# Attention's reciprocal row sums sent through DRAM, and the output copied and scaled in two separate steps

## The chip, the core and the metric

The kernel runs on one core of a Trainium2 chip. The metric is the device time of one execution in microseconds (us). The core's engines are named as a profile names them: PE is TensorE (PEld its weight loads), DVE is VectorE, ACT is ScalarE, POOL is GpSimd, SP is SyncE, which only issues transfers here. Each engine works through its own list of instructions in order and waits on semaphores for the others. A transfer is issued by SP or by POOL, and then runs on the 16 DMA engines of the core.

## What is computed

One layer of a hybrid network over 1024 latent tokens of width 1024 and 256 context tokens: a half-step feed-forward, then a short convolution and a grouped-query attention in parallel, merged through gates, then a second feed-forward. The change lies in the attention, where 8 query heads of width 128 share 2 key and value heads:

```python
def gqa_attend(q, k, v):
    s = jnp.einsum('btkgd,blkd->bkgtl', q, k, preferred_element_type=jnp.float32) * (HEAD_DIM ** -0.5)
    p = jax.nn.softmax(s, axis=-1).astype(v.dtype)
    return jnp.einsum('bkgtl,blkd->btkgd', p, v)
...
    k_all = jnp.concatenate([k_c, k_l], axis=1)
    v_all = jnp.concatenate([v_c, v_l], axis=1)
    o_l = latent_attention(q_l, k_all, v_all)

    x = x + ml[5] * merge_branches(y_conv_l, o_l, gt_l, w_branch_conv[layer],
                                   w_branch_attn[layer], w_out[layer])
```

Each query attends to 256 + 1024 = 1280 keys. The softmax's division by the row sum may be done after the product with the values, and so it is here.

## The kernel before

**Products in three parts.** Everything is float32. A factor is split into a high part and a rest (`split`: ScalarE writes the rounded high part with a cast, VectorE, or GpSimd where it is named, subtracts it for the rest), and each product is three matmuls, high x high, high x rest, rest x high.

**Units.** The attention runs in 16 units: 8 heads times two chunks of 512 queries (`C0`, `C1`). A unit has four query tiles (`qt`) of 128 queries. `scores` makes the scores of one tile in three PSUM banks (512 + 512 latent keys, 256 context keys), VectorE takes their maxima (`m3`, then `nm`), ScalarE the exponentials with the row sums as a by-product (into `pl` and `pc`), and VectorE adds the three part sums into one column of `rsum`. So after the fourth tile `rsum` holds 128 x 4 row sums, one query on each partition.

**Values.** The second half of a unit has ten key tiles (`kt`) of 128 keys. `turn(kt)` transposes four 128 x 128 blocks of exponentials on TensorE into one PSUM bank, and `split` makes `pts` of it. `values(kt)` multiplies it with the value tile and adds up in the PSUM bank `po` over all ten tiles. The result has the head's 128 dimensions on the partitions and the 512 queries along the row, so that scaling it takes the reciprocal sums as a row, the same on all partitions.

**The output, as it was.** `output` takes the reciprocals of `rsum` (`rinv`, 128 x 4), spreads them into rows by four transposes on TensorE of a broadcast column (into a PSUM bank of the same kind that `turn` uses), copies `po` to SBUF on ScalarE (`of`), multiplies `of` by that bank on VectorE, and splits the product into the operand `o` of the later branch product.

**What sets the order.** The loop at the end of the stage (`for n, u in enumerate(units)`) interleaves three threads on TensorE: the scores of unit n, in eight half steps; the turns and values of unit n - 1 (`seconds`, one `rest` a step, with values three turns behind, `AHEAD = 3`); and filler products of the convolution and merge branches (`fillers`, `FILLS` steps per unit). While `in_order[0]` is set, TensorE keeps exactly this order. The other engines' lists are set by a scheduler with a cost model of its own, which takes what is ready by its times. The last value product of a unit falls into the fifth half step of the unit after next; between it and the next unit's first value product stand one filler step and one turn.

**Buffers.** `t` banks of PSUM: two, shared by the turns and (before) the spread reciprocals. `po`: one. Row tiles in SBUF (`ttile`, 512 wide): eleven, for queries, gates, `of` and others. Weights of the fillers are loaded to `raw` (three), cast by ScalarE, and subtracted by GpSimd into `wc`; the next weight load on SyncE's list waits for a free `raw`. Query loads (`o<-qd`) stand on the same list, and GpSimd subtracts for the rest of the queries as well (`qs`).

Of the kernel before, what the change touches and what calls it, by code (L numbers as in the profile page):

```python
# [9 lines left out]
F32 = mybir.dt.float32  # L10
# [8 lines left out]
P = 128  # L19
# [7 lines left out]
NQ = 8  # L27
# [24 lines left out]
def tile_dit_layer(  # L52
# [29 lines left out]
    class Engine:  # L82


        def __init__(self, engine):
            self.engine = engine
# [10 lines left out]
    act, dve, pool, pe, sp = (Engine(e) for e in (nc.scalar, nc.vector, nc.gpsimd, nc.tensor, nc.sync))  # L97
# [7 lines left out]
    dram = ctx.enter_context(tc.tile_pool(name="dram", bufs=1, space=DRAM))  # L105
# [3 lines left out]
    def uniq(s):  # L109
        n_tiles[0] += 1  # L110
        return f"{s}_{n_tiles[0]}"

    def atile(name, shape=(P, SLOT), dt=F32):
        return apool.tile(list(shape), dt, tag="A", name=uniq(name))

    def ttile(name, n=512, dt=F32):
        t = tpool.tile([P, 512], dt, tag="t", name=uniq(name))
        return t[:, :n]

    def small(name, n, dt=F32):  # L120
        return spool.tile([P, n], dt, tag=f"s{n}_{name}", name=uniq(name))

    def ps_s(n=512):
        return psum.tile([P, 512], F32, tag="s", name=uniq("ps"), bufs=5)[:, :n]

    def ps_t(n=512):
        return psum.tile([P, 512], F32, tag="t", name=uniq("pt"), bufs=2)[:, :n]

    def ps_o(n=512):
        return psum.tile([P, 512], F32, tag="o", name=uniq("po"), bufs=1)[:, :n]  # L130

    def matmul(out, w, x, start, stop, pinned=False, on=False):

        inst = pe.matmul(out, w, x, start=start, stop=stop, skip_group_check=on)
        if pinned or in_order[0]:
            tc.keep_in_program_order(inst)

    def transpose(out, in_, pinned=False):
        n = in_.shape[0]
        inst = pe.transpose(out, in_, ident[:n, :n])  # L140
        if pinned or in_order[0]:
            tc.keep_in_program_order(inst)
# [37 lines left out]
    def col(name, k=0):  # L180
        o = voff[name] + k
        return cols[:, o : o + 1]
# [8 lines left out]
    def split(src, hi, lo, lo_eng=None, hi_eng=None):  # L191

        if hi_eng is dve:
            dve.tensor_copy(out=hi, in_=src)
        else:
            act.copy(out=hi, in_=src)
        (lo_eng or dve).tensor_sub(out=lo, in0=src, in1=hi.bitcast(F32))
# [25 lines left out]
    def mm3(ps, terms, k0=0, k1=None):  # L223

        last = len(terms) - 1
        for i, (wh, wl, xh, xl) in list(enumerate(terms))[k0:k1]:
            matmul(ps, wh, xh, start=(i == 0), stop=False)
            matmul(ps, wh, xl, start=False, stop=False)
            matmul(ps, wl, xh, start=False, stop=(i == last))
# [565 lines left out]
    class OutColumns(Winograd):  # L795
# [71 lines left out]
        def seconds(self, j):  # L867

            u, v = self.uc[j]
            b = ttile("b")  # L870
            dve.tensor_add(out=u, in0=u, in1=self.product(6))
            dve.tensor_add(out=v, in0=u, in1=self.product(7))
            dve.tensor_sub(out=b, in0=v, in1=self.product(4))
            return b
# [268 lines left out]
    def scaled(k, pt):  # L1143
        act.copy(out=xs(k, C0), in_=pt)
        dve.tensor_mul(out=h0[k % 4][:, k // 4], in0=pt, in1=pr)
# [18 lines left out]
    pr = ttile("pr")  # L1164
# [200 lines left out]
    for j in range(NH):  # L1365
# [3 lines left out]
        u, c = half1.next_first()  # L1369
# [109 lines left out]
    for i in range(KD):  # L1479
        u = atile("u")  # L1480
# [5 lines left out]
        for ch, bg, gc in mixed():  # L1486
# [3 lines left out]
            o = ch[1]  # L1490
            y = ttile("y")
            dve.tensor_scalar(out=y, in0=u[:, o : o + 512], scalar1=col("w1", i), scalar2=None, op0=ALU.mult)
            for j in (0, 2):
# [3 lines left out]
                    out=ya, in0=u[:, a + j - 1 : b + j - 1], scalar=col(f"w{j}", i), in1=ya, op0=ALU.mult, op1=ALU.add  # L1497
# [135 lines left out]
    def v_tile(kt):  # L1633
        if kt < 2:
            return v_ctx[:, kt], v_ctx[:, 2 + kt]
        return tuple(t[:, (kt - 2) % 4] for t in v_lat[(kt - 2) // 4])
# [194 lines left out]
    queries, o_parts = {}, {}  # L1831
# [46 lines left out]
    def conv_out(ch, j):  # L1878
# [10 lines left out]
        sp.dma_start(out=zd[j, :, o : o + 512], in_=g)  # L1889
        yield  # L1890

    class Unit:
        def __init__(self, hd, ch):
            self.hd, self.ch, self.g = hd, ch, hd // (NQ // NKV)
# [11 lines left out]
        def scores(self, qt):  # L1906

            g = self.g
            qh, ql = (t[:, qt * P : (qt + 1) * P] for t in self.qs)
            m3, nm, rs = small("m3", 3), small("nm", 1), small("rs", 3)  # L1910
            pl, parts = atile("pl"), []
            self.pl.append(pl)

            def keys(n, k, dst):
                ps = ps_s(n)
                mm3(ps, [(qh, ql, *k)])
                dve.reduce_max(out=m3[:, len(parts) : len(parts) + 1], in_=ps, axis=AX.X)
                parts.append((dst, ps))

            keys(512, [t[:, :512] for t in k_lat[g]], pl[:, :512])  # L1920
            yield
            keys(512, [t[:, 512:] for t in k_lat[g]], pl[:, 512:])
            keys(CT, [k_ctx[:, 2 * g + v] for v in range(2)], self.pc[:, qt])
            i = 8 * (self.hd // 2 * 2 + self.ch[1] // 512) + 4 * (self.hd % 2) + qt
            y = q_scale[:, i : i + 1]
            dve.tensor_reduce(out=nm[:], in_=m3[:], axis=AX.X, op=ALU.max, negate=True)
            dve.tensor_mul(out=nm[:], in0=nm[:], in1=y)
            for j, (dst, ps) in enumerate(parts):
                act.activation(out=dst, in_=ps, func=AF.Exp, bias=nm[:], scale=y, accum_out=rs[:, j : j + 1])
            dve.reduce_sum(out=self.rsum[:, qt : qt + 1], in_=rs[:], axis=AX.X)  # L1930
            yield

        def turn(self, kt):
# [6 lines left out]
            split(pt, pts[:, 0], pts[:, 1])  # L1940
            return pts

        def values(self, kt, pts):
            if kt == 0:
                self.po = ps_o()
            po = self.po
            vh, vl = (v[:, self.g * HD : (self.g + 1) * HD] for v in v_tile(kt))
            matmul(po, vh, pts[:, 0], start=(kt == 0), stop=False)
            matmul(po, vh, pts[:, 1], start=False, stop=False)
            matmul(po, vl, pts[:, 0], start=False, stop=(kt == 9))  # L1950

        def output(self):
            rinv = small("rinv", 4)
            of, o = ttile("of"), o_parts[self.hd, self.ch]
            dve.reciprocal(out=rinv[:], in_=self.rsum[:])
            pr = ps_t()
            for qt in range(4):
                transpose(pr[:, qt * P : (qt + 1) * P], rinv[:, qt : qt + 1].to_broadcast([P, P]))
            act.copy(out=of, in_=self.po)
            dve.tensor_mul(out=of, in0=of, in1=pr)  # L1960
            split(of, o[:, 0], o[:, 1])

    def seconds():

        turned = []

        def value():
            u, kt, pts = turned.pop(0)
            u.values(kt, pts)
            if kt == 9:  # L1970
                u.output()

        for u in units:
            for kt in range(10):
                turned.append((u, kt, u.turn(kt)))
                if len(turned) > AHEAD:
                    value()
                yield
        while turned:
            value()  # L1980
            yield

    merged = OutColumns([tuple(w_out[0][:, d * P : (d + 1) * P] for d in (e, e + 1)) for e in range(0, KD, 2)])

# [41 lines left out]

    units = [Unit(hd, ch) for ch in (C0, C1) for hd in range(NQ)]
    rest, fill = seconds(), fillers()
    in_order[0] = True
    for n, u in enumerate(units):  # L2030
# [155 lines left out]
    for j in range(NH):  # L2186
        if j > 1:
            run(late_steps, 3)
        u, c = fast.next_first()
# [76 lines left out]
```

## Time and profile before

| What | us |
|---|---|
| Median of 3 runs | 2643.44 (2640.8 to 2643.78) |
| The profiled execution | 2642.17 |
| Its span, first to last instruction | 2640.4 |
| PE busy | 2593.3 (98%) |
| DVE busy | 2072.1 (78%) |
| ACT busy | 1207.4 (46%) |
| POOL busy | 545.1 (21%) |

In a row of the order of time the columns are the start, the length, the engine, the line in the code, the operation, output<-inputs, sizes, and the number of equal instructions that were merged. In brackets stands how long the engine was idle before it, and what it waited for. Nearly all instructions carry line 90, since one helper issues them; they are told apart by the names of their tiles. Matmuls overlap, and a row of several is as long as from the first start to the last end, so distances on PE are read from start to start. In a row by tile the three durations are the shortest, the median and the longest in ns.

### The profile page before, as it was taken

To read this page: it belongs to the slowest core of one execution; us is meant where nothing else is said; L and a number is where in the kernel's file an instruction comes from. 1 tells how busy PE (TensorE), PEld (TensorE's weight loads), DVE (VectorE), ACT (ScalarE), POOL (GpSimd) and SP (SyncE) were. 2 spreads that over 40 slices of the span, in tenths; PEclk is the share of its full clock that TensorE was granted. 3 is DMA by queue.
4 is the path that set the end of the run, shared out by engine and by line. 5 is a ranking of instruction groups with operands and counts; after the bars stand their busy time and mean duration, and the time that the engine had idled before them with its cause. 6 is when DMAs were issued, how large, how long until landed. Compare 5 with 4: busy or idle time off the path is not lost.

```text
span 2640.4 us, 36969 instructions
## 1 busy us (share of the span) xinstructions
PE 2593.3 (98%) x13313; PEld 2189.6 (83%) x13313; DVE 2072.1 (78%) x3463; ACT 1207.4 (46%) x2388; POOL 545.1 (21%) x374
## 2 busy tenths in 40 slices
PE   8999999999999999999999999999999999999998
PEld 5788998888788878888998788888887888888888
DVE  5888879887887899888687766677788777667885
ACT  5623543233444643323456666666447423334444
POOL 1144011121110044232310011111030443321110
PEclk9999999999999999999999999999999999999999
DMA  8665754437974345444536222122434664227851
GB/s 271 223 188 175 231 157 137 128 108 265 292 173 116 116 158 173 135 128 127 176 116 216 88 69 72 55 70 69 138 110 136 195 185 138 88 76 271 215 104 65
DMA packets 373456, 393.08 MB, mean 149 GB/s; under 512 B 16655, under 2 KB 255385, under 8 KB 373273
## 3 DMA queue, kind: packets, MB, share of 16 engines
q1 hardware_dynamic: 364248, 373.43, 44.1%
q0 software_dynamic: 9024, 17.30, 4.1%
q8 instruction: 104, 1.70, 0.3%
q14 instruction: 80, 0.65, 0.1%
HBM read 313.07 MB, written 77.59 MB: 148 GB/s over the span
## 4 chain that ended last, share of the span: by engine, by line
PE 84%; DVE 8%; ACT 4%; DMA 2%; issue 2%; POOL 0%; SPq 0%; DVEq 0%; POOLq 0%; ACTq 0%
PE ps L90 70%; PE po L90 8%; PE pt L90 7%; ACT pl L90 1%; DVE pts L90 1%; DVE r L90 1%; DMA raw<-in_ffn_w_in_dram 1%; DVE wl L90 1%; DVE m L90 1%; ACT r L90 0%; ACT pts L90 0%; ACT wl L90 0%; DVE v L90 0%; DVE u L90 0%; DMA xtok<-in_ctx_dram 0%
## 5 line engine op out<-in xcount | busy, mean ns | idle before, releaser
L90 PE MATMUL ps<-r,wl 128*128 128x512 f32 x5496 | 1267.6, 390 | 8.6 <-DVE wl L90 3.5
L90 PEld LDWEIGHTS ps<-r,wl 128*128 128x128 f32 x5496 | 1026.6, 188 | 223.4 <-DVE wl L90 5.0
L90 ACT CAST wl<-s 128x512 fp32r<-128x512 f32 x266 | 164.4, 620 | 371.4 <-PE ps L90 258.1
L90 ACT CAST wl<-raw 128x512 fp32r<-128x512 f32 x298 | 184.1, 620 | 236.4 <-PE ps L90 140.3
L90 DVE TENSOR_TENSOR wl<-raw,wl 128x512 fp32r<-128x512 f32 x296 | 215.1, 730 | 70.4 <-ACT wl L90 69.2
L90 POOL TENSOR_TENSOR s<-raw 128x512 f32<-128x512 f32 x68 | 98.5, 1448 | 792.5 <-DMA raw<-in_ffn_w_in_dram 384.7
L90 DVE TENSOR_TENSOR wl<-s,wl 128x512 fp32r<-128x512 f32 x266 | 231.0, 870 | 22.4 <-ACT wl L90 21.2
L90 POOL TENSOR_TENSOR s<-raw,s 128x512 f32<-128x512 f32 x68 | 102.6, 1508 | 369.3 <-DVE wl L90 361.4
L90 DVE TENSOR_REDUCE m<-ps 128x1 f32<-128x512 f32 (+1 forms) x192 | 111.0, 596 | 59.3 <-PE ps L90 59.1
L90 DVE SCALAR_TENSOR_TENSOR macc<-rawm,silu_c,macc 128x512 f32<-128x512 f32 x168 | 141.8, 860 | 8.5 <-DMA rawm<-in_w_mod_dram 8.0
L90 DVE TENSOR_TENSOR u<-u,ps 128x512 f32<-128x512 f32 x183 | 124.3, 679 | 26.1 <-PE ps L90 25.9
L90 ACT CAST pts<-pt 128x512 fp32r<-128x512 f32 x160 | 93.6, 587 | 101.7 <-PE pt L90 101.1
L90 PE MATMUL ps<-tw,r 128*128 128x256 f32 x1008 | 125.2, 285 | 3.7 <-DVE tw L90 3.5
L90 DVE TENSOR_TENSOR pts<-pt,pts 128x512 fp32r<-128x512 f32 x160 | 109.5, 685 | 23.8 <-ACT pts L90 21.6
L90 PEld LDWEIGHTS ps<-tw,r 128*128 128x128 f32 x1008 | 122.2, 192 | 4.8 <-DVE tw L90 4.7
L90 ACT CAST rh<-hid 128x512 fp32r<-128x512 f32 x132 | 80.9, 620 | 95.1 <-PE ps L90 86.1
L90 PE MATMUL ps<-rh,wl 128*128 128x512 f32 x360 | 122.0, 389 | 0.0
L90 PE MATMUL po<-pts,v 128*128 128x512 f32 x384 | 120.0, 422 | 0.0
L90 ACT ACTIVATE pl<-ps,nm,qscale 128x512 f32<-128x512 f32 x128 | 98.6, 775 | 43.5 <-DVE nm L90 43.2
L90 POOL TENSOR_TENSOR s<-raw,raw 128x512 f32<-128x512 f32 x74 | 111.6, 1508 | 8.1 <-issue 2.7
L90 PE MATMUL ps<-kl,qs 128*128 128x512 f32 x384 | 110.3, 395 | 2.9 <-ACT pl L90 2.7
L90 PE MATMUL ps<-y,wc 128*128 128x512 f32 x384 | 105.3, 395 | 1.9 <-DVE g L90 1.9
(366 smaller groups left out, 4630.8 us busy)
## 6 DMA issues: line engine op xcount, KB each, us to landing
raw<-in_ffn_w_in_dram SPq DMA_DIRECT2D x128, 512.0 KB
raw<-in_ffn_w_out_dram SPq DMA_DIRECT2D x72, 512.0 KB
rawm<-in_w_mod_dram SPq DMA_DIRECT2D x128, 256.0 KB
raw<-in_w_in_dram SPq DMA_DIRECT2D x53, 512.0 KB
hid<-hd SPq DMA_DIRECT2D x40, 512.0 KB
ws<-in_ffn_w_out_dram POOLq DMA_DIRECT2D x30, 512.0 KB, 6.4
ucd<-uc SPq DMA_DIRECT2D x26, 512.0 KB
hd<-c SPq DMA_DIRECT2D x39, 256.0 KB
```

What stands on the lines that cost most here:

```text
L90: inst = getattr(self.engine, name)(*args, **kw)
```

## The change

Three things change. The reciprocals are taken at the end of a unit's scores, and GpSimd stores the 512 numbers to DRAM, into a row of `rsd`, in the order of the queries. At the unit's fifth value step GpSimd fetches this row back to all 128 partitions (`inv`). `output` only copies `po`, and the multiplication and the split are written two value steps later (`scaled`, at `kt == 1` of the next unit), with `inv` in SBUF as the second operand. The four transposes and their bank are not used any more.

```diff
+    rsd = dram.tile([NQ, 2, 512], F32, name="rsd")
...
             dve.reduce_sum(out=self.rsum[:, qt : qt + 1], in_=rs[:], axis=AX.X)
+            if qt == 3:
+                rinv = small("rinv", 4)
+                dve.reciprocal(out=rinv[:], in_=self.rsum[:])
+                pool.dma_start(out=rsd[self.hd, self.ch[1] // 512].rearrange("(t p) -> p t", p=P), in_=rinv[:])
...
+        def fetch_inverse(self):
+            self.inverse = ttile("inv")
+            pool.dma_start(out=self.inverse, in_=rsd[self.hd, self.ch[1] // 512].partition_broadcast(P))
...
         def output(self):
-            rinv = small("rinv", 4)
-            of, o = ttile("of"), o_parts[self.hd, self.ch]
-            dve.reciprocal(out=rinv[:], in_=self.rsum[:])
-            pr = ps_t()
-            for qt in range(4):
-                transpose(pr[:, qt * P : (qt + 1) * P], rinv[:, qt : qt + 1].to_broadcast([P, P]))
-            act.copy(out=of, in_=self.po)
-            dve.tensor_mul(out=of, in0=of, in1=pr)
+            self.of = ttile("of")
+            act.copy(out=self.of, in_=self.po)
+
+        def scaled(self):
+            of, o = self.of, o_parts[self.hd, self.ch]
+            dve.tensor_mul(out=of, in0=of, in1=self.inverse)
             split(of, o[:, 0], o[:, 1])
...
-        turned = []
+        turned, ended = [], []
 
         def value():
             u, kt, pts = turned.pop(0)
+            if kt == 4:
+                u.fetch_inverse()
             u.values(kt, pts)
             if kt == 9:
                 u.output()
+                ended.append(u)
+            elif kt == 1 and ended:
+                ended.pop().scaled()
...
         while turned:
             value()
             yield
+        ended.pop().scaled()
```

The order on the engines, as built. TensorE at the fourteenth output, before: the last value product (`po`), the spread reciprocals (`pt` from `rinv`), a filler product (`ps`), the next turn.

```order
L90 MATMUL po_17587<-pts_17753,v_13346 128x512 x2
L90 MATMUL po_17587<-pts_17753,v_13347 128x512
L90 MATMUL pt_17841<-ident,rinv_17838 128x128 x4
L90 MATMUL ps_17728<-o_14801,wc_17256 128x512 x2
L90 MATMUL ps_17728<-o_14801,wc_17257 128x512
L90 MATMUL pt_17853<-ident,pl_17424 128x128
```

The same place with the change:

```order
L90 MATMUL po_17562<-pts_17736,v_13346 128x512 x2
L90 MATMUL po_17562<-pts_17736,v_13347 128x512
L90 MATMUL ps_17711<-o_14796,wc_17243 128x512 x2
L90 MATMUL ps_17711<-o_14796,wc_17244 128x512
L90 MATMUL pt_17826<-ident,pl_17409 128x128
```

The four transposes are gone, and the rest of TensorE's list in the stage is as it was. VectorE at the same output, before: the split of the turn ahead (`pts`), the scaling, the split of the output (`o`), the split of the next turn, two maxima of the scores.

```order
L90 TENSOR_TENSOR pts_17832<-pt_17827,pts_17832 128x512
L90 TENSOR_TENSOR of_17839<-of_17839,pt_17841 128x512
L90 TENSOR_TENSOR o_17030<-of_17839,o_17030 128x512
L90 TENSOR_TENSOR pts_17858<-pt_17853,pts_17858 128x512
L90 TENSOR_REDUCE m_3195_17818<-ps_17865 128x1
L90 TENSOR_REDUCE m_3195_17818<-ps_17870 128x1
```

With the change:

```order
L90 TENSOR_TENSOR pts_17815<-pt_17810,pts_17815 128x512
L90 TENSOR_TENSOR of_17821<-of_17821,inv_17669 128x512
L90 TENSOR_TENSOR pts_17831<-pt_17826,pts_17831 128x512
L90 TENSOR_REDUCE m_3198_17801<-ps_17838 128x1
L90 TENSOR_TENSOR o_17009<-of_17821,o_17009 128x512
L90 TENSOR_REDUCE m_3198_17801<-ps_17843 128x1
```

The scaling keeps its place, with the fetched row as its second operand, and the output's split goes behind the next turn's split and a maximum; on ScalarE the cast of `o` goes behind the cast of `pts` likewise. GpSimd around the sixth and seventh unit, before: the rests of the queries (`qs`) and of the fillers' weights (`wc`).

```order
L90 TENSOR_TENSOR qs_15382<-o_15379,qs_15381 128x512
L90 TENSOR_TENSOR wc_15289<-raw_15287,wc_15288 128x1024
L90 TENSOR_TENSOR qs_15654<-o_15651,qs_15653 128x512
L90 TENSOR_TENSOR wc_15508<-raw_15506,wc_15507 128x1024
L90 TENSOR_TENSOR qs_15928<-o_15925,qs_15927 128x512
```

With the change:

```order
L90 TENSOR_TENSOR qs_15373<-o_15370,qs_15372 128x512
L90 DMA inv_15473<-rsd 128x512
L90 DMA rsd<-rinv_15448 128x4x1
L90 TENSOR_TENSOR wc_15290<-raw_15288,wc_15289 128x1024
L90 TENSOR_TENSOR qs_15643<-o_15640,qs_15642 128x512
L90 DMA inv_15754<-rsd 128x512
L90 TENSOR_TENSOR wc_15507<-raw_15505,wc_15506 128x1024
L90 DMA rsd<-rinv_15720 128x4x1
L90 TENSOR_TENSOR qs_15915<-o_15912,qs_15914 128x512
```

In every unit a fetch stands right behind a `qs`, and a store follows, behind the fetch or behind a `wc`. SyncE's list is the same as before.

## The prediction

> **What bounds the kernel now.** I read the chain that ended last first, then the busy times by stage, then the order of time around one of the sixteen places that the change touches.
>
> ```profile
> PE 84%; DVE 8%; ACT 4%; DMA 2%; issue 2%; POOL 0%; SPq 0%; DVEq 0%; POOLq 0%; ACTq 0%
> ```
>
> TensorE (PE) carries 84% of the chain; GpSimd (POOL) and all queues carry nothing. Next the attention stage and all behind it (start:end, length, then busy us and count of PE, PEld, DVE, ACT, POOL, granted clock, DMA share, GB/s):
>
> ```profile
> 1430.00:1867.00 437.00, 423.99 (x2271) 348.52 (x2270) 307.72 (x653) 279.90 (x640) 60.84 (x32) 1.00 0.22 71
> 1867.00:2640.00 773.00, 762.31 (x3532) 636.26 (x3530) 587.03 (x889) 320.26 (x557) 171.96 (x122) 1.00 0.50 147
> ```
>
> In the stage TensorE idles 437.00 - 423.99 = 13 us, VectorE (DVE) 129, ScalarE 157; the clock is full and the DMA engines are 22% busy. So the stage ends when TensorE is through its list, and what is saved there is handed on: in the 773 us behind it TensorE idles 10.7 us only. Where TensorE stands still for others shows at an output; this is the fourteenth:
>
> ```profile
> 1827.55 0.60 PE L90 MATMUL pt<-ident,rinv 128*128 128x128 f32 x4
> 1827.91 0.94 PE L90 MATMUL ps<-o,wc 128*128 128x512 f32 x3
> 1828.12 0.61 ACT L90 COPY of<-po 128x512 f32<-128x512 f32 x1
> 1828.27 0.69 DVE L90 TENSOR_TENSOR pts<-pt,pts 128x512 fp32r<-128x512 f32 x1 [0.32 <-ACT pts L90]
> 1829.02 0.66 PE L90 MATMUL pt<-ident,pl 128*128 128x128 f32 x4 [0.17 <-DVE pts L90]
> 1829.43 0.94 PE L90 MATMUL po<-pts,vc 128*128 128x512 f32 x3
> ```
>
> The four `rinv` transposes take one of the two `t` banks, so the next turn (`pt<-ident,pl`) must wait for the bank of the turn before, which VectorE frees at 1828.96. The third output has no such wait:
>
> ```profile
> 1535.78 0.60 PE L90 MATMUL pt<-ident,rinv 128*128 128x128 f32 x4
> 1536.13 0.94 PE L90 MATMUL ps<-y,wc 128*128 128x512 f32 x3
> 1536.91 0.60 PE L90 MATMUL pt<-ident,pl 128*128 128x128 f32 x4
> 1537.27 0.96 PE L90 MATMUL po<-pts,vc 128*128 128x512 f32 x3
> ```
>
> From start to start: 0.35 us for the transposes, 0.78 for the filler, 0.36 for the turn, 1.49 in all. The fourteenth output takes 1.88, so 0.39 us goes into the bank, more than the 0.17 that the row names as idle.
>
> **Part one, the transposes go.** Alone they are worth 16 x 0.355 = 5.7 us:
>
> ```profile
> L90 PE MATMUL pt<-ident,rinv x64: 270/273/273, 1479.7 to 1867.1; 128*128 128x128 f32 x64
> ```
>
> With the bank also free, the next value product can begin 0.78 + 0.36 = 1.14 us after the old start of the transposes, unless ScalarE's copy of `po` (one bank) is late. I allow 0.05 us between the copy's end and TensorE. Fourteenth output: the copy ends at 1828.73, 1.18 in, so 1.23 instead of 1.88: 0.65 saved. The fourth is the first of eight of this kind (numbers 4, 5, 6, 8, 10, 12, 13 and 14; the last is shown above):
>
> ```profile
> 1562.48 0.60 PE L90 MATMUL pt<-ident,rinv 128*128 128x128 f32 x4
> 1562.94 0.61 ACT L90 COPY of<-po 128x512 f32<-128x512 f32 x1
> 1564.25 0.94 PE L90 MATMUL po<-pts,vc 128*128 128x512 f32 x3
> ```
>
> Here 1.77 becomes 1.14: 0.63. Eight times 0.64 is 5.1 us. Outputs 3, 15 and 16 lose only the transposes: 3 x 0.35 = 1.05. The first two outputs:
>
> ```profile
> 1479.73 0.60 PE L90 MATMUL pt<-ident,rinv 128*128 128x128 f32 x4
> 1481.34 0.60 ACT L90 COPY of<-po 128x512 f32<-128x512 f32 x1
> 1482.77 0.94 PE L90 MATMUL po<-pts,vc 128*128 128x512 f32 x3
> 1507.57 0.60 PE L90 MATMUL pt<-ident,rinv 128*128 128x128 f32 x4
> 1510.25 0.58 ACT L90 COPY of<-po 128x512 f32<-128x512 f32 x1
> 1510.88 0.97 PE L90 MATMUL po<-pts,vc 128*128 128x512 f32 x3 [1.43 <-ACT of L90]
> ```
>
> The first goes from 3.04 to 2.26 (the copy's end plus 0.05): 0.78. The second already waits for the copy: nothing. So far 5.1 + 1.05 + 0.78 = 6.9 us.
>
> Outputs 7, 9 and 11 stay open. There TensorE stands still twice soon after the output:
>
> ```profile
> 1643.31 2.72 DVE L90 TENSOR_TENSOR o<-of,o 128x512 fp32r<-128x512 f32 x1 [0.76 <-POOL qs L90]
> 1643.08 2.40 POOL L90 TENSOR_TENSOR wc<-raw,wc 128x1024 fp32r<-128x1024 f32 x1
> 1647.37 0.63 PE L90 MATMUL pt<-ident,pl 128*128 128x128 f32 x4 [0.92 <-DVE pts L90]
> 1649.84 0.96 PE L90 MATMUL ps<-kl,qs 128*128 128x512 f32 x3 [0.44 <-ACT pl L90]
> 1700.97 0.66 PE L90 MATMUL pt<-ident,pl 128*128 128x128 f32 x4 [0.64 <-DVE pts L90]
> 1703.65 0.96 PE L90 MATMUL ps<-kl,qs 128*128 128x512 f32 x3 [0.63 <-ACT pl L90]
> 1754.93 0.63 PE L90 MATMUL pt<-ident,pl 128*128 128x128 f32 x4 [1.03 <-DVE pts L90]
> 1757.40 0.96 PE L90 MATMUL ps<-kl,qs 128*128 128x512 f32 x3 [0.45 <-ACT pl L90]
> ```
>
> In the new order VectorE does `pts` ahead of `o`, which should end the first wait of each pair. The second hangs on the sum of VectorE's work up to the exponentials, which is the same as before. Their own savings are 0.35 + 0.65 + 0.35 = 1.35, the six waits 4.1: between 0 and 5.5. If the second wait takes everything back, nothing is left; I take about a third, 1.7, nearer to the 1.35.
>
> **Part two, 32 transfers are added on GpSimd.** The nearest rows:
>
> ```profile
> L90 POOL DMA_DIRECT2D ws<-in_ffn_w_out_dram x36: 1194/1222/1442, 682.0 to 2541.1; - x36
> DMA to landing us min/median/max: 5.6/6.5/10.1
> L90 DVE RECIPROCAL rinv<-rsum x16: 166/178/182, 1441.4 to 1842.5; 128x4 f32<-128x4 f32 x16
> 1615.00 0.61 ACT L90 COPY of<-po 128x512 f32<-128x512 f32 x1
> 1616.21 1.30 POOL L90 TENSOR_TENSOR qs<-o,qs 128x512 fp32r<-128x512 f32 x1 [10.13 <-ACT qs L90]
> SPq L90 <- POOL wc L90: 146.0, 17, 20.1
> ```
>
> An issue costs GpSimd 1.2 us: 32 x 1.2 = 39 us beside 61 busy ones in a stage of 437. A store of 512 single numbers is not in the trace; I take 1.2 us too, by the nearest row, up to a few times that at worst. The fetch stands behind `qs`: in the unit of the sixth output (the two rows with a time) it issues near 1617.5 and lands, at the longest landing of 10.1, by 1629. Outputs are (1867.1 - 1479.7) / 15 = 25.8 us apart, so it is used near 1615.6 + 25.8 = 1641.4: 12 us to spare. The last store can issue after 1842.5, its fetch waits for it, and two landings of 6.5 with two issues of 1.2 end at 1858, before output 16. Cost 0.
>
> The store is the wait that is added on GpSimd: it waits for the reciprocal, and where a `wc` subtraction is next in the list, that starts up to 1.2 us later. SyncE's next weight load waits for `wc` (last row), and the next query load stands behind it. These loads are for a later unit, and that cover hides the push; without it ScalarE, which has the query's split in its list ahead of `pts`, would stand still for up to 1.2 us in that unit.
>
> **Part three, the product moves and changes its operand.** `of*inv` stands in VectorE's list where `of*pt` stood, so it hides as before, 0.68 us. It reads two SBUF operands now instead of SBUF and PSUM:
>
> ```profile
> L90 DVE TENSOR_TENSOR of<-of,pt x16: 677/677/689, 1482.8 to 1869.5; 128x512 f32<-128x512 f32 x16
> L90 DVE TENSOR_TENSOR o<-of,o x16: 677/1290/2892, 1485.4 to 1870.9; 128x512 fp32r<-128x512 f32 x16
> L90 DVE TENSOR_TENSOR wl<-ws,wl x35: 682/686/693, 749.9 to 2546.1; 128x512 fp32r<-128x512 f32 x35
> ```
>
> The form with PSUM is never stretched; `o`, of two SBUF operands beside GpSimd's subtractions, is, by 0.6 us in the median and 2.2 at most; beside GpSimd's DMA issues (`wl<-ws,wl`) nothing is. At the sixth output GpSimd begins `qs` 0.6 us after the copy's end, when `of*inv` would have begun; I take 0, with 0 to 1.3 us (one `qs`) per output as the bounds, and 16 x 1.3 = 20.8 us in all.
>
> **Sum.** 6.9 + 1.7 = 8.6 us. The profiled execution took 2642.17 us (span 2640.4, 1.8 around it): 2642.2 - 8.6 = 2633.6. The median of the three runs is 2643.44, 1.3 more, inside their own spread of 3 us.
>
> **Rivals.**
> - The saving is taken back within the unit: the score products still wait for ScalarE's exponentials and VectorE's maxima, as the second waits above do, and a TensorE that is 0.64 us early waits 0.64 us longer. For it: the second output gains nothing, for just that reason. Against it: VectorE idles 129 us in the stage, and only a few waits of this kind show. Between none and half of the sum is left: 2638 to 2642.
> - Slower: `of*inv` and GpSimd lock each other out. If `qs` or `wc` is running at most outputs when the copy ends, the product waits for its end, and `pts`, the maxima and so the turns stand behind it. At 1.3 us on the path at each output this is 2642.2 - 8.6 + 20.8 = 2654.4; it decides from 8.6 / 16 = 0.54 us each. For it: the stretched `o` rows. Against it: GpSimd is busy for 61 of the stage's 437 us, and with `pts` ahead of `o` one SBUF pair less stands before the next turn. The Trainium skill (SBUF — State Buffer, section SBUF: two separate sides) says that a VectorE operation with two SBUF inputs and a GpSimd operation that reads SBUF share a port pair, and that the one which starts first holds it for its whole instruction. The trace agrees: the `o` that began at 1643.31 ended at 1646.03, about one normal length after the end of the `wc` of 1643.08.
> - The fetch is late: four-byte stores so slow that the inverse lands more than 12 us after the time above. Then VectorE stands still at every output, by 16 times the excess: 2 us excess gives 2665. The order of instructions excludes that the transposes stay or that the fetch is issued only at the output.
> - More: all waits at outputs 7, 9 and 11 go, and others like them: 13 us or more, below 2629.
>
> **Chances.** Forecast 0.67 (2629 to 2638), taken back 0.18, locked out 0.08, late 0.03, more 0.04. A measurement tells 0.2%, some 5.3 us, from no change: faster is below 2638.2, slower above 2648.7. Faster 0.67 + 0.04 = 0.71; same 0.18 + 0.02 of mild lock-outs = 0.20; slower 0.06 + 0.03 = 0.09. The range 2629 to 2641 holds the forecast and most of the taken-back case, and leaves out 0.04 + 0.08 + 0.03 and 0.04 at that case's far end.
>
> **What the profile will show.** Right: from the last value product of a unit to the next unit's first, some 0.35 us less at three outputs and 0.6 at eight; `of<-of,inv` near 0.68 us; the stage shorter by 7 to 10 us and the rest unchanged. Wrong: `of<-of,inv` with a mean over 1.2 us, a DMA wait in front of it, waits on `pl` or `pts` that grow, or query loads that land later.

## The result, and the profile after

| | us |
|---|---|
| Before, median of 4 runs | 2642.61 (2640.80 to 2643.78) |
| With the change, median of 4 runs | 2655.88 (2654.01 to 2661.21) |
| Ratio | 1.0055, 95% interval 1.0043 to 1.0067 |
| Profiled execution with the change, its span | 2655.56, 2653.6 |

The change makes the kernel 13 us slower. The forecast was 2633.6 with a range of 2629 to 2641, so the time lies outside it, on the other side of no change.

Chain of waits of the changed kernel, by engine and by line:

```profile
PE 82%; DVE 7%; DMA 5%; ACT 3%; issue 2%; SPq 1%; POOL 0%; DVEq 0%; ACTq 0%; POOLq 0%
PE ps L90 69%; PE po L90 7%; PE pt L90 6%; DMA o<-qd 2%; DVE wl L90 1%; DVE r L90 1%; DMA g<-gcd 1%; DMA raw<-in_ffn_w_in_dram 1%; DMA rawm<-in_w_mod_dram 1%; SPq L90 1%; ACT pl L90 1%; DVE m L90 1%; DVE pts L90 0%; DVE u L90 0%; DMA y<-yd 
```

DMA went from 2% to 5%, and the query loads (`o<-qd`) stand in the chain. Two stretches of the changed kernel (start:end, length, then busy us and count of PE, PEld, DVE, ACT, POOL, granted clock, DMA share, GB/s), the stage as it was cut before and up to its own last output copy:

```profile
1430.00:1867.00 437.00, 411.66 (x2136) 337.89 (x2135) 295.51 (x639) 270.62 (x624) 80.44 (x62) 0.98 0.33 79
1430.00:1881.20 451.20, 425.86 (x2212) 349.57 (x2211) 304.94 (x652) 278.65 (x637) 80.99 (x63) 0.98 0.33 78
```

The kernel before, up to its last output copy:

```profile
1430.00:1867.80 437.80, 424.79 (x2276) 349.23 (x2275) 308.52 (x654) 280.70 (x640) 60.84 (x32) 1.00 0.22 70
```

The stage alone is 13.4 us longer, which is the whole difference. TensorE idles 25.3 us in it instead of 13.0, and it is 1.1 us longer busy although 64 transposes are gone: its clock is granted at 0.98. The DMA engines are 33% busy instead of 22% while they move 78 GB/s instead of 70, so half as much time again goes for a tenth more bytes.

The added transfers (shortest, median and longest issue in ns; landing in us; the first two rows are the store):

```profile
L90 POOL DMA_DIRECT2D rsd<-rinv x16: 755/766/826, 1440.9 to 1856.9; - x16
DMA to landing us min/median/max: 8.6/9.7/11.6
...
L90 POOL DMA_DIRECT2D inv<-rsd x16: 552/567/600, 1455.9 to 1867.9; - x16
L90 DVE TENSOR_TENSOR of<-of,inv x16: 680/684/1908, 1485.0 to 1882.9; 128x512 f32<-128x512 f32 x16
...
DMA to landing us min/median/max: 3.3/3.7/8.1
```

Two KB need 9.7 us to land; the fetch of 256 KB needs 3.7. Now one such store and the loads beside it (order of time of the changed kernel, around the sixth output; the engine is the third column):

```profile
1610.72 0.76 POOL L90 DMA_DIRECT2D rsd<-rinv  x1 [9.93 <-DVE rinv L90]
...
1613.93 0.38 SPq L90 DMA_DIRECT2D raw<-in_w_branch_conv_dram  x1
1614.41 0.53 SPq L90 DMA_DIRECT2D o<-qd  x1
...
1625.38 0.62 ACT L90 CAST qs<-o 128x512 fp32r<-128x512 f32 x1 [2.57 <-DMA o<-qd]
...
1629.63 0.78 ACT L90 ACTIVATE pl<-ps,nm,qscale 128x512 f32<-128x512 f32 x1 [2.14 <-DVE nm L90]
...
1630.55 0.96 PE L90 MATMUL ps<-kl,qs 128*128 128x512 f32 x3 [1.24 <-ACT pl L90]
```

The same stretch in windows of 1 us (last two columns: DMA share, GB/s):

```profile
1612.00:1613.00 1.00, 1.00 (x8) 0.91 (x7) 0.94 (x3) 0.39 (x1) 1.00 (x1) 1.00 0.18 2
...
1616.00:1617.00 1.00, 1.00 (x6) 0.79 (x6) 0.16 (x1) 0.86 (x3) 0.00 (x0) 1.00 0.01 2
...
1618.00:1619.00 1.00, 1.00 (x6) 0.83 (x5) 1.00 (x3) 0.59 (x1) 0.00 (x0) 1.00 0.63 60
1619.00:1620.00 1.00, 1.00 (x6) 0.84 (x5) 0.61 (x3) 0.32 (x1) 0.00 (x0) 1.00 0.52 28
...
1621.00:1622.00 1.00, 1.00 (x6) 0.82 (x6) 0.51 (x2) 1.00 (x5) 0.00 (x0) 1.00 0.71 24
...
1623.00:1624.00 1.00, 1.00 (x5) 0.83 (x6) 0.65 (x2) 0.00 (x0) 0.00 (x0) 1.00 1.09 332
1624.00:1625.00 1.00, 1.00 (x9) 0.92 (x8) 0.00 (x0) 0.00 (x0) 0.00 (x0) 1.00 1.02 380
```

In the kernel before, the same weight load and query load (order of time of SyncE):

```profile
1606.10 0.38 SPq L90 DMA_DIRECT2D raw<-in_w_branch_conv_dram  x1
1606.58 0.53 SPq L90 DMA_DIRECT2D o<-qd  x1
```

and its windows of 1 us:

```profile
1607.00:1608.00 1.00, 1.00 (x8) 0.86 (x7) 0.57 (x1) 1.00 (x3) 0.00 (x0) 1.00 0.45 110
1608.00:1609.00 1.00, 1.00 (x6) 0.82 (x5) 0.12 (x1) 1.00 (x4) 0.00 (x0) 1.00 0.99 301
1609.00:1610.00 1.00, 1.00 (x7) 0.82 (x6) 0.20 (x2) 0.66 (x3) 0.00 (x0) 1.00 1.11 366
```

Before, the loads run at 300 GB/s within two us of their issue and are through by 1611. With the change they are issued at 1613.9 to 1614.9, and the core moves 60 GB/s or less until 1622. The store began at 1610.72 and, at the median landing, was through at 1620.4. Its own 2 KB are the 2 GB/s in the window from 1612, two us after its issue; what takes long comes behind that, up to the landing. So the store does not only take long itself: the transfers beside it nearly stand still. ScalarE then waits at the query's split (`qs<-o`), the exponentials (`pl`) behind it in its list come late, and TensorE waits for them. The waits in 1430 to 1860 of the changed kernel (who, for what, us, times, longest):

```profile
ACT qs L90 <- DMA o<-qd: 20.3, 7, 4.0
PE ps L90 <- ACT pl L90: 11.6, 9, 2.6
...
ACT y L90 <- DMA y<-yd: 7.6, 5, 3.1
PE po L90 <- ACT of L90: 6.2, 2, 4.2
```

And of the kernel before:

```profile
PE pt L90 <- DVE pts L90: 5.2, 10, 1.3
ACT qs L90 <- DMA o<-qd: 4.3, 3, 2.7
...
PE ps L90 <- ACT pl L90: 2.7, 5, 0.6
...
PE po L90 <- ACT of L90: 1.4, 1, 1.4
```

The longer waits cost twice. After the wait for `pl` of 2.64 us that ends at 1658.75, the column ahead of the DMA share, the granted clock, goes down in the changed kernel:

```profile
1659.00:1660.00 1.00, 1.00 (x7) 0.73 (x7) 0.25 (x1) 1.00 (x4) 0.00 (x0) 1.00 0.21 61
1660.00:1661.00 1.00, 1.00 (x8) 0.90 (x7) 0.97 (x4) 0.21 (x2) 0.00 (x0) 0.65 0.06 16
1661.00:1662.00 1.00, 1.00 (x4) 0.81 (x3) 0.77 (x3) 1.00 (x3) 0.00 (x0) 0.50 0.00 0
1662.00:1663.00 1.00, 1.00 (x3) 0.66 (x3) 0.10 (x1) 1.00 (x5) 0.00 (x0) 0.50 0.00 0
1663.00:1664.00 1.00, 1.00 (x6) 0.94 (x5) 0.33 (x2) 0.45 (x2) 0.00 (x0) 0.64 0.00 0
```

TensorE is busy again, but at half clock for 3.4 us. This comes with four waits of the changed kernel, of 4.17, 1.99, 2.64 and 1.74 us (with the first it begins within the wait and lasts 6.8 us), and with none of those of 1.31 us or less. One minus the clock, added up over these stretches of the stage, comes to 8.5 us with the change and to 0 before.

### The profile page after: what moved, and what is told of

Its sections match the earlier page's. It is cut to its first block, busy times and chain, and to the rows that moved or that the text cites. A ratio compares the mean times of both kernels' runs of the same rounds, so it can differ in the third digit from the quotient of the medians.

```text
span 2653.6 us, 36915 instructions
## 1 busy us (share of the span) xinstructions
PE 2594.4 (98%) x13249; PEld 2191.1 (83%) x13249; DVE 2070.4 (78%) x3463; ACT 1206.4 (45%) x2388; POOL 567.0 (21%) x406
## 4 chain that ended last, share of the span: by engine, by line
PE 82%; DVE 7%; DMA 5%; ACT 3%; issue 2%; SPq 1%; POOL 0%; DVEq 0%; ACTq 0%; POOLq 0%
PE ps L90 69%; PE po L90 7%; PE pt L90 6%; DMA o<-qd 2%; DVE wl L90 1%; DVE r L90 1%; DMA g<-gcd 1%; DMA raw<-in_ffn_w_in_dram 1%; DMA rawm<-in_w_mod_dram 1%; SPq L90 1%; ACT pl L90 1%; DVE m L90 1%; DVE pts L90 0%; DVE u L90 0%; DMA y<-yd 0%
## 5 line engine op out<-in xcount | busy, mean ns | idle before, releaser
L90 ACT CAST pts<-pt 128x512 fp32r<-128x512 f32 x160 | 93.7, 587 | 93.1 <-PE pt L90 92.6
```

The lines of the kernel that those rows point to most:

```text
L90: inst = getattr(self.engine, name)(*args, **kw)
```

## The experiments

In the first four, theory S is the one just read from the trace; P, F and O are its rivals: pushed lists, the fetch, the new order on ScalarE and VectorE. All times are medians; the kernel before measured 2642.75 beside the first four, 2642.30 beside the second four, 2641.63 beside experiments 9, 11 and 12, and 2642.31 beside experiment 10. Waits are those in 1430 to 1860 where nothing else is said.

**1. The same store, in 16-byte pieces.**

```diff
-   pool.dma_start(out=rsd[self.hd, self.ch[1] // 512].rearrange("(t p) -> p t", p=P), in_=rinv[:])
+   pool.dma_start(out=rsd[self.hd, self.ch[1] // 512].rearrange("(p t) -> p t", p=P), in_=rinv[:])
...
-   dve.tensor_mul(out=of, in0=of, in1=self.inverse)
+   by_tile = lambda a, s: a.rearrange(s, t=4)
+   dve.tensor_mul(out=by_tile(of, "q (t p) -> q t p"), in0=by_tile(of, "q (t p) -> q t p"),
+                  in1=by_tile(self.inverse, "q (p t) -> q t p"))
```

> The changed kernel, with the row sums' reciprocals stored in the order in which they lie in SBUF: each partition writes its four numbers as 16 contiguous bytes (128 pieces in place of 512 of 4 bytes), and the product reads the inverse through a strided view that puts the columns right. When the store issues, what it waits for and the order on every engine stay. Theory S (the 512 four-byte pieces occupy the DMA engines, the query loads beside them land late, and ScalarE stands at the query's split): the store lands in about 3 to 5 us instead of 9.7, ScalarE's wait for the query load falls from 20.3 us to about the 4.9 of before, and the time to about 2634, the forecast; anything from 2630 to 2640 bears it out. Theory P (GpSimd stands at the store until the reciprocal is there, so its subtraction and with it SyncE's next loads issue late): that wait is unchanged, 2654 to 2657. Theory F (the fetch of 256 KB): unchanged, 2654 to 2657. Theory O (the new order on ScalarE and VectorE costs): 2654 to 2657, or more if the strided read is slow; the product's row, 0.68 us, tells.

Measured: 2637.89, ratio 0.9982 (0.9973 to 0.9991) to the kernel before, 18 us below the changed kernel. Store, its landing, and the product in this run:

```profile
L90 POOL DMA_DIRECT2D rsd<-rinv x16: 543/552/624, 1441.6 to 1837.3; - x16
...
DMA to landing us min/median/max: 1.7/1.7/4.2
...
L90 DVE TENSOR_TENSOR of<-of,inv x16: 1062/1085/2310, 1482.2 to 1863.4; 128x512 f32<-128x512 f32 x16
...
ACT qs L90 <- DMA o<-qd: 4.8, 3, 2.3
```

The landing falls from 9.7 to 1.7 us, the query wait from 20.3 to 4.8, and the clock in the stage is 1.00 again. Bytes, queue and order are those of the changed kernel, and GpSimd still waits for the reciprocal (93.7 us in 13 waits, against 85.1 in 12), so P, F and O fall as causes of the loss. The strided read makes the product 0.40 us longer, and VectorE hides it.

**2. Only the fetch.**

```diff
-   pool.dma_start(out=rsd[self.hd, self.ch[1] // 512]...
+   if self.hd + self.ch[1] == 0:
+       pool.dma_start(out=rsd[self.hd, self.ch[1] // 512]...
...
-   pool.dma_start(out=self.inverse, in_=rsd[self.hd, self.ch[1] // 512].partition_broadcast(P))
+   pool.dma_start(out=self.inverse, in_=rsd[0, 0].partition_broadcast(P))
```

> The changed kernel, but only the first unit stores its reciprocals, and all sixteen units fetch that one row (so fifteen units are scaled by the first one's sums). All reciprocals, fetches and products stay. S: about 2634 (2630 to 2640). P: the same, since GpSimd no longer waits for reciprocals; the 16-byte store tells S from P. F: 2654 to 2657, as the fetches are all there. O: 2654 to 2657.

Measured: 2637.48, ratio 0.9982 (0.9973 to 0.9990). Fifteen stores in four-byte pieces cost 2655.88 - 2637.48 = 18.4 us.

**3. Neither store nor fetch.**

```diff
-   pool.dma_start(out=rsd[self.hd, self.ch[1] // 512].rearrange("(t p) -> p t", p=P), in_=rinv[:])
...
-   self.inverse = ttile("inv")
-   pool.dma_start(out=self.inverse, in_=rsd[self.hd, self.ch[1] // 512].partition_broadcast(P))
+   self.inverse = k_lat[self.g][0][:, :512].bitcast(F32)
```

> The changed kernel with neither store nor fetch: the output is multiplied by a resident tile of keys in place of the inverse (so it is not normalised), and one temporary less is taken per unit. What is left of the change is that the transposes are gone and that the product and the split come later. S and P: 2632 to 2638, the forecast with nothing beside it, and within 2 us of the kernel that only fetches. F: the same here, but some 20 us faster than the kernel that only fetches. O: 2654 to 2657.

Measured: 2633.97, ratio 0.9961 (0.9948 to 0.9975): 8.8 us less than before, where the forecast for these parts was 8.6. What is left of the waits in 1430 to 1860:

```profile
PE ps L90 <- ACT pl L90: 4.3, 5, 1.8
...
PE po L90 <- ACT of L90: 3.0, 2, 2.0
```

TensorE's turns no longer wait for `pts` (5.2 us in ten waits before); the waits for `pl` and for `of` have grown by 1.6 us each. The kernel that only fetches takes 3.5 us more, where S and P had expected less than 2; since it still has one store in four-byte pieces, and the two intervals overlap by a hair, the price of the fetch is somewhere between 0 and this.

**4. The kernel before with the store alone.**

```diff
+            if qt == 3:
+                rinv = self.rinv = small("rinv", 4)
+                dve.reciprocal(out=rinv[:], in_=self.rsum[:])
+                pool.dma_start(out=rsd[self.hd, self.ch[1] // 512].rearrange("(t p) -> p t", p=P), in_=rinv[:])
...
-            dve.reciprocal(out=rinv[:], in_=self.rsum[:])
...
-                transpose(pr[:, qt * P : (qt + 1) * P], rinv[:, qt : qt + 1].to_broadcast([P, P]))
+                transpose(pr[:, qt * P : (qt + 1) * P], self.rinv[:, qt : qt + 1].to_broadcast([P, P]))
```

> The kernel before plus one thing: the reciprocals are taken at the end of the scores and stored to DRAM as in the changed kernel, and nothing reads them. Transposes, the product with PSUM and the order of the output stay. S and P: the whole loss without the gain, 13 us between the kernels plus the 8.6 that were to be saved: 2655 to 2665. F and O: 2641 to 2645, as before.

Measured: 2666.00, ratio 1.0090 (1.0076 to 1.0103), 1 us above the range of S and P. A store that nobody reads costs 23 us in the old order:

```profile
DMA to landing us min/median/max: 8.6/9.6/12.9
```

```profile
ACT qs L90 <- DMA o<-qd: 24.7, 10, 4.3
...
PE pt L90 <- DVE pts L90: 14.7, 14, 2.3
...
ACT y L90 <- DMA y<-yd: 12.0, 5, 6.0
```

With the transposes still there, it is the turns (`pt`) that wait most. So the cause is shown twice: taken away from the changed kernel, and added to the kernel before.

**5. The query asked for earlier, load and split.**

```diff
-            if half == 5 and n < len(units) - 1:
+            if half == 3 and n < len(units) - 1:
                 fetch_query(n + 1, pool)
```

> The changed kernel, four-byte stores and all, with the next unit's query load and split asked for two eighths of a unit earlier (half 3 in place of half 5). Theory Q (the stores hurt through this one load, at which ScalarE stands): ScalarE's wait for it falls from 20.3 us to under 5, and the time goes from 2655.9 to 2638 to 2645. Theory T (the DMA engines' time is taken from every load, and another one, the convolution's inputs or the weights, takes the query's place as the late one): the wait moves to y or wc, and the time stays at 2650 or above.

Measured: 2709.21, ratio 1.0246 (1.0232 to 1.0261), which neither theory had. The edit moves ScalarE's split as well as the load, and the load stays behind a weight load in SyncE's list: nine of its fourteen loads behind the first store issue within 4 us of a store, against four of fourteen in the changed kernel, and the split needs it 6 us sooner. The wait it was meant to end grew, in 1430 to 1880, from 20.3 to 54.1 us:

```profile
ACT qs L90 <- DMA o<-qd: 54.1, 8, 8.9
```

**6 and 7. The same edit with the 16-byte store, and on the kernel before**, as controls.

> The kernel with the 16-byte store, with the query asked for at half 3 as well. If its remaining 4.8 us of waiting for the query load stand on the path, 2632 to 2636; if that wait is covered, 2636 to 2640 as with the 16-byte store alone. Were it slower than 2640, the two query tiles that are then held longer would be the cause.

> The kernel before with the query asked for at half 3 and nothing else, as the control for the two kernels that do this. ScalarE's waits for the query load in the stage are 4.3 us there; at most these go: 2638 to 2643.

Measured: 2637.36 with the 16-byte store, ratio 0.9975 (0.9963 to 0.9986), and 2642.46 on the kernel before, ratio 0.9999 (0.9990 to 1.0008). Both lie in their ranges. So asking earlier is harmless by itself, and the 67 us above the kernel before in experiment 5 are again the store's: what it costs depends on which load falls beside it and how soon that load is needed.

**8. The same 512 pieces in four stores.**

```diff
-            if qt == 3:
-                rinv = small("rinv", 4)
...
+            one = slice(qt, qt + 1)
+            dve.reciprocal(out=self.rinv[:, one], in_=self.rsum[:, one])
+            row = rsd[self.hd, self.ch[1] // 512, qt * P : (qt + 1) * P]
+            pool.dma_start(out=row.rearrange("(p o) -> p o", o=1), in_=self.rinv[:, one])
```

> The changed kernel with the same 512 four-byte pieces per unit in four stores of 128, each issued when its quarter of the rows has its sum (64 stores in all, and 64 small reciprocals in place of 16). The number of pieces is the same, but they come in bursts of a quarter. Theory B (one burst stands ahead of the query load and is waited out): a store lands in 3 to 5 us, the query wait falls to a third or less, 2638 to 2646. Theory T (the sum of the pieces' time counts, however they are spread): the query wait and the time stay, 2653 to 2658. GpSimd then issues 48 more stores and stands at four reciprocals per unit; if that holds up its subtractions, SyncE's loads come late and the time is above 2658.

Measured: 2687.74, ratio 1.0165 (1.0151 to 1.0179). Theories B and T fall by the landing and by the time:

```profile
L90 POOL DMA_DIRECT2D rsd<-rinv x64: 538/538/624, 1422.1 to 1888.0; - x64
...
DMA to landing us min/median/max: 7.1/8.6/15.0
```

A store of 128 four-byte pieces takes 8.6 us, nearly as long as one of 512, while 128 pieces of 16 bytes took 1.7. So it is not the number of pieces. The time is that of the third case, above 2658, but its reason doesn't show: SyncE's wait for GpSimd's `wc` is 84.2 us here and 136.0 in the changed kernel, while ScalarE's wait for the query load is 30.8. What the two slow stores share is 128 pieces side by side in each 512 bytes of DRAM; the store of experiment 1 has 32. That gave theory A below.

**9 and 10. Four-byte pieces set apart in DRAM.** The kernel of experiment 2, with a store in the other fifteen units to a tensor of its own, with the numbers 64 bytes apart (a last dimension of 16 in `apart`), then 16 bytes (of 4).

```diff
+    apart = dram.tile([NQ, 2, 512, 16], F32, name="apart")
...
+                    row = apart[self.hd, self.ch[1] // 512, :, 0]
+                    pool.dma_start(out=row.rearrange("(t p) -> p t", p=P), in_=rinv[:])
```

> The kernel that only fetches (one row for all units), plus a store of 512 four-byte pieces in each of the other fifteen units, to a second DRAM tensor that nothing reads, where the numbers lie 64 bytes apart instead of side by side. Theory A (four-byte pieces that fall side by side into the same stretch of DRAM wait for one another: 512 or 128 pieces land in 8 to 10 us either way, 16-byte pieces in 1.7): the store lands in 2 to 4 us, and the time is about that of the kernel that only fetches, 2636 to 2641. Theory W (each four-byte piece is slow wherever it goes): it lands in 8 to 10 us, and the time is 2653 to 2658 as in the changed kernel.

> As the run with the numbers 64 bytes apart, but 16 bytes apart (the starts lie as those of the 16-byte pieces do, and three of four numbers between them aren't written). One row is fetched for all units again. If what counts is how many pieces share a stretch of DRAM, with 64 bytes apart free and side by side dear, this lies between: 32 pieces share 512 bytes and 4 share 64 bytes, as with the 16-byte pieces, which landed in 1.7 us; so 2 to 4 us and 2636 to 2641. If a piece of less than some 64 bytes that shares its stretch with any other is what is slow: 6 us or more, and 2645 or above.

Measured: 2638.01, ratio 0.9983 (0.9974 to 0.9992), with 64 bytes, and 2635.58, ratio 0.9976 (0.9966 to 0.9986), with 16, a little under its range. The store at 64 bytes, and the window of 1 us that holds the packets of the one issued at 1605.01:

```profile
L90 POOL DMA_DIRECT2D apart<-rinv x15: 755/764/784, 1471.9 to 1839.1; - x15
...
DMA to landing us min/median/max: 2.2/2.2/4.5
...
1606.00:1607.00 1.00, 1.00 (x9) 0.95 (x9) 1.00 (x3) 0.12 (x1) 1.00 (x1) 1.00 0.18 2
```

The one at 16 bytes lands in 2.2 us too. Same pieces, same bytes, same issue of 0.76 us, same wait of GpSimd for the reciprocal, and the same share of 0.18 at 2 GB/s while the packets pass: apart from one another they cost nothing that these runs can tell. Theory W falls, and theory A has what it forecast. One thing is not separated: wherever a store was fast, every piece began at a multiple of 16 bytes, and side by side only every fourth does. Whether the neighbours count or these starts, no run here shows. The result also takes away what was left of P, since GpSimd's list is pushed here as in the changed kernel.

**11. The load alone asked for earlier**, at half 2, the split left at half 5.

```diff
...
+            if half == 2 and n < len(units) - 1:
+                load_query(n + 1)
             if half == 5 and n < len(units) - 1:
                 fetch_query(n + 1, pool)
```

`load_query` holds the load that was in `fetch_query`.

> The changed kernel with the query load alone asked for three eighths of a unit earlier (half 2); its split stays at half 5, unlike in the run that moved both. If the store stops the transfers for its 9.7 us and the load needs only to be asked for so early that it lands before the split all the same: the wait for the query falls from 20.3 us to under 8, and the time to 2638 to 2648. If the load cannot start earlier because SyncE stands at the weight load ahead of it, or what stands behind it is late instead: 2650 to 2660.

Measured: 2654.78, ratio 1.0045 (1.0030 to 1.0060), as the changed kernel. The wait for the query falls only to 15.2 us, and others are longer than in the changed kernel (7.6 us for `y`, 4.4 for `pts`):

```profile
ACT qs L90 <- DMA o<-qd: 15.2, 6, 4.6
...
ACT y L90 <- DMA y<-yd: 8.7, 4, 6.1
PE pt L90 <- DVE pts L90: 8.3, 4, 6.9
```

The load was asked for earlier, but in most units it did not start earlier. From its issue to the split it has clearly more time in seven of the sixteen units; in the ninth, for one, it stands behind a weight load in SyncE's list as before and issues 11.0 us ahead of the split in both kernels. So this run doesn't tell what a load that is early everywhere would save. That the query load is not the only way of the loss is seen elsewhere: ScalarE's wait for `y` is 2.8 us before, 7.6 with the change and 12.0 in experiment 4.

**12. The store on ScalarE's queue.**

```diff
-   pool.dma_start(out=rsd[self.hd, self.ch[1] // 512].rearrange("(t p) -> p t", p=P), in_=rinv[:])
+   act.dma_start(out=rsd[self.hd, self.ch[1] // 512].rearrange("(t p) -> p t", p=P), in_=rinv[:])
```

> The changed kernel with the four-byte store issued by ScalarE on its own queue in place of GpSimd; the fetch stays. Theory A or W (the pieces themselves): landing near 9 us and the same stop of the other transfers, 2653 to 2660. Theory G (GpSimd's queue makes such a store slow): the store lands in 2 to 4 us and the time is about 2638. In both, ScalarE stands until the reciprocal is there, which may add up to 16 times 1 us.

Measured: 2651.74, ratio 1.0036 (1.0022 to 1.0050), 1.3 us under the range of A and W, with 15.8 us of waiting for the query. Its landing is not in the trace. Most of the loss stays, so GpSimd's queue is not its cause. The interval overlaps with that of the changed kernel, so it stays open whether the 4 us less are real.

**The better version.** With the 16-byte store (experiment 1) the kernel is faster than both, by 0.2% against the kernel before and by 0.7% against the changed one; with the query also asked for earlier it is not distinguishably better.

## Why the prediction was wrong

- **The bound: right.** TensorE's list sets the end of the stage, and behind the stage nothing changed: the 13.4 us of the stage are the 13 us of the total.
- **Part one: right, in sum and nearly in kind.** Without the transfers, 8.8 us by the medians against 8.6. Up to the last output copy the profile has 1867.8 - 1861.3 = 6.5, but its first query load issues at 1399.7 against 1397.3 before, ahead of all that the change touches, so within the stage it is 9.0. From the start of a unit's last value product to that of the next unit's first, experiment 3 has 0.79 us less at the first output, nothing at the second, 0.44 at outputs 3 and 15, and 0.65 to 0.68 at the eight, where 0.78, 0, 0.35 and 0.64 were forecast; the changed kernel has the same from the second output on, within 0.05. At outputs 7, 9 and 11 it is 1.58 in all, near their own savings of 1.35. That some of the other waits there would be won as well was a guess; the waits for `pts` went, and those for `pl` and `of` took 3.2 us back.
- **Part two: here it failed.** The step is the "Cost 0" of the added transfers, and under it "A store of 512 single numbers is not in the trace; I take 1.2 us too, by the nearest row, up to a few times that at worst". The issue is in fact cheaper, 0.77 us, and the landing is 9.7. Even that landing was harmless for what was asked of it: the fetch was in time, and no product waited for `inv` in the changed kernel. What was never asked is what the store does to the transfers that run beside it. They nearly stood still, and that cost 18.4 us (fifteen stores, experiment 2), beside a saving of 8.8. The nearest row was of the wrong kind: an issue of rows of 512 numbers says nothing of numbers written one by one, side by side.
- **The cover of the query load** was named, and the place of the damage with it: ScalarE with the query's split ahead of `pts`. But its price was bounded by GpSimd's push, 1.2 us, where ScalarE waited for the load itself, up to 4.0 us at a time and 20.3 in all. The push was free, as experiments 9 and 10 show.
- **Part three: right.** The product with two SBUF operands takes 684 ns in the median against 677. It is stretched at three of the sixteen outputs, to 1.9 us, each time beside a `wc` of GpSimd that began 1 us earlier: 3 x 1.22 = 3.7 us, inside the bounds that were given. Experiment 1 has three such rows too and is 18 us faster, so they are not the loss.
- **The rivals.** The lock of VectorE and GpSimd would have given 2654.4, close to what was measured, but by accident: it needs 1.3 us on the path at all sixteen outputs, and the product's row has 1.2 us at three of sixteen. The late fetch had the right cause, slow four-byte stores, with the wrong victim; its condition, more than 12 us, was never met. The rival that was missing is a transfer that costs by what it does to the transfers beside it rather than by its own wait.
- **What the profile was to show:** "query loads that land later" was among the signs of being wrong, and it is the one that came, with the waits on `pl` behind it.

## What to carry to other kernels

A small transfer off the critical path is not free because its issue is short and its result is in time: look also at the loads that run beside it, and at which engine stands still in order when one of them is late. Don't write single numbers side by side to DRAM; let each partition write its numbers as one piece, and put the order right where it is read. And when an operation has no row in the trace, a bound taken from a row of another shape is no bound; the forecast should then hold a case in which the unknown price falls on others.

## What the hardware showed that was not expected

- Side by side in DRAM, 512 four-byte pieces landed in 9.7 us and 128 in 8.6; 16 or 64 bytes apart, 512 landed in 2.2; 128 pieces of 16 bytes in 1.7. The Trainium skill (DMA: Bandwidth & Descriptors, section Rules for kernel authors) says that a last dimension that isn't contiguous becomes one descriptor per element, and advises to rearrange it. The advice agrees with experiment 1; the reason does not reach, since at 16 and 64 bytes there were as many single elements and they cost nothing that could be measured. What in the chip makes the store slow, and whether it goes by neighbours or by where a piece begins, is not shown by these runs.
- While the store shown above was under way, the loads beside it ran at 60 GB/s or less, where the same loads ran at 300 and more before. The store's own packets pass as quickly as those of a fast one.
- A pause of TensorE of 1.6 us or more was mostly, not always, followed by half clock (16 of 23 such pauses in the stages of the changed kernel and of experiments 1, 3, 4 and 8), for some 3.4 us after a short pause; none of 1.52 us or less was in these five, but in experiment 2 one of 1.49 us with another of 1.24 right behind it was; pauses of 1.74, 1.99, 2.64 and 4.17 us did it in the changed kernel, pauses of 1.98 and 1.72 us in experiment 1 did not. The Trainium skill (TensorE: Matmul & The Clock Gate, section Part 1: The HAM clock gate) has a gate at half clock that looks at windows of about 3.4 us that run on their own, and gives an idle window of that length as what closes it. The length of the slow stretch agrees, and so do windows that run on their own: in the changed kernel the slow stretches begin at 1482.81, 1516.94, 1660.30 and 1769.53, which are 10, 42 and 32 times 3.41 us apart. That would fit that equal pauses differ; but here half that idle time was enough.
